# Moving weight splitting to VectorE, folding epsilon into a 65th column, and a third product tile for the conv

## The chip, the cores and the metric

The kernel runs on one core of one Trainium2 chip. The metric is the device time of one execution in microseconds (us). Before the change the runs took 1763.9, 1765.36 and 1767.11 us, with a median of 1765.36. The profiled execution took 1766.28 us, and its trace spans 1764.5 us from the first to the last instruction.

## The reference, cut to what matters

One block works on x of 1024 tokens by 1024 channels, in fp32. Four branches start from one normalised input:

```
h = rms_norm(x, g1);  z = h @ w_in            # 2048 glu, 3 x 1024 q k v, 2048 gate columns
a = a_val * sigmoid(a_gate)                    # glu
a = silu(rms_norm(causal_depthwise_conv(a, conv_w, conv_b), g))     # 31 taps
q = rms_norm(q per head of 64) * 64**-0.5;  k = rms_norm(k per head of 64)
o = dilated attention of q, k, v (16 heads, three dilations mixed)
x = x + (g_a * (a @ w_conv_out) + g_b * (o @ w_attn_out)) @ w_out
x = x + (silu(u_gate) * u_val) @ w_down        # u: conv of 3 taps of rms_norm(x) @ w_up
rms_norm(x, g) = x * rsqrt(mean(x * x) + 1e-6) * g
```

## The kernel before, in words

**Products in two halves.** A matrix product keeps fp32 precision by splitting each operand into a high part, rounded to the matmul type, and a low part, the rest. `split` (lines 78 to 81) does it: ScalarE copies the high part (line 80), and the engine that is passed as `by` subtracts to get the low part (line 81; VectorE where nothing is passed). Three matmuls then stand for one: high by high, high by low, low by high. `wsplit` (line 88) does this for weights. Weights come into a ring of four raw tiles named `raw` and leave as tiles `hi_...` and `lo_...`.

**The glu stage** (up to about 200 us) makes the 2048 glu columns in eight pairs of 128 value and 128 gate columns. Pairs 0 and 1 use plain products (`first_pair`, line 368). Pairs 2 to 7 use a scheme with seven instead of eight block products: the operands are sums and differences of blocks. VectorE forms those of the input once (lines 507 and 517 make the `forms` t1 to t4). For each pair, `pair_weights` (line 376) stages and splits the value weights, and `pair_sums` (line 385) makes four sums of 128x512 of the weights (line 390) and splits them. All this subtracting and adding is GpSimd's, as is the low part of pair 1's weights (line 494). `pair_first` and `pair_rest` (line 554) issue the products, through line 124 to 126, with the results named `uxz` and `uy`.

**The q, k and v stage** (about 175 to 475 us) makes six blocks of 512 columns, in order q, k, v, q, k, v, each over eight tiles of 128 tokens. A tile takes 24 matmuls (`gemm_tok`, line 144). For q and k `qkv_head` then does: ScalarE squares the tile (line 655), VectorE sums 64 squares for each of 8 heads (line 656), VectorE scales the sums by 1/64 and adds epsilon (line 104 in `rstd_of`), GpSimd raises to the power −1/2 (line 105), and VectorE scales the tile (line 659, tile `qn`). `qkv_tail`, three tiles later in the program, transposes on TensorE (line 667, `qt`), splits and stores. A v tile is split into a tile of a ring of four named `t4` and stored to HBM.

**The conv of 31 taps** runs beside that stage: six of eight channel blocks on VectorE (`by_dve`, line 624, one tap an instruction), two (3 and 6) as ScalarE products (line 615) that GpSimd adds up (line 616), with two product tiles in turn.

**What sets the order.** Each engine works through one queue in order. In a few places the order is the program's own (the manual schedules: the start, the attention, the change to the second half). Elsewhere, and so in the places of this change, a planner orders the instructions of each engine from a model of their costs (`schedule_with_timeline_sim` where the kernel is built).

Of the kernel before, what the change touches and what calls it, by code (L numbers as in the profile page):

```python
# [13 lines left out]
F32 = mybir.dt.float32  # L14
F32R = mybir.dt.float32r
AF = mybir.ActivationFunctionType
ALU = mybir.AluOpType
AX = mybir.AxisListType
# [3 lines left out]
P = 128  # L22
D = 1024
T = 1024
KT = D // P
H = 16
DH = 64
DFF = 2816
FT = DFF // P
CW = 31  # L30
FW = 3
EPS = 1e-6
# [21 lines left out]
def block_kernel(ctx: ExitStack, tc: tile.TileContext, x, g1, g2, pack, mask,  # L54
                 w_ch, w_qkv, w_co, w_ao, w_o, w_up, w_down, out):
    nc = tc.nc
    act, dve, pool, pe, sp = nc.scalar, nc.vector, nc.gpsimd, nc.tensor, nc.sync
# [17 lines left out]
    mhalf = cst.tile([P, 8], F32, name="mhalf")  # L75
    qkg = cst.tile([P, 1], F32, name="qkg")

    def split(hi, lo, src, by=dve):

        act.activation(hi, src, AF.Copy)  # L80
        by.tensor_tensor(out=lo, in0=src, in1=hi.bitcast(F32), op=ALU.subtract)  # L81
# [6 lines left out]
    def wsplit(src, name, by=dve):  # L88
        hi = wp.tile([P, 1024], F32R, tag="whi", bufs=4, name=f"hi_{name}")[:, : src.shape[1]]
        lo = wp.tile([P, 1024], F32R, tag="wlo", bufs=4, name=f"lo_{name}")[:, : src.shape[1]]  # L90
        split(hi, lo, src, by)
        return hi, lo
# [9 lines left out]
    def rstd_of(dst, ssq, n, tmp):  # L102

        dve.tensor_scalar(tmp, ssq, 1.0 / n, EPS, op0=ALU.mult, op1=ALU.add)
        pool.tensor_tensor(out=dst, in0=tmp, in1=mhalf[:, : tmp.shape[1]], op=ALU.pow)
# [23 lines left out]
    def four(t):  # L129
        return t.rearrange("p (a b) -> p a b", b=P)  # L130
# [166 lines left out]
    with tc.tile_pool(name="ph0", bufs=1, reuse_waits="tile") as p0:  # L297
# [77 lines left out]

        def pair_weights(c):
            v = stage(w_ch[c], f"v{c}")
            return v, wsplit(v, f"v{c}", pool)

        def pair_first(xz, w):  # L380
            for i, o in enumerate(xz):
# [3 lines left out]
        def pair_sums(c, v):  # L385
            g = stage(w_ch[8 + c], f"g{c}")
            s = wp.tile([P, 1024], F32, tag="raw", bufs=4, name=f"s12_{c}")
            a11, a12, a21, a22 = v[:, 0:512], v[:, 512:], g[:, 0:512], g[:, 512:]
            s1, s2 = s[:, 0:512], s[:, 512:]
            add_ = lambda o, a, b, op: pool.tensor_tensor(out=o, in0=a, in1=b, op=op)  # L390
            add_(s1, a21, a22, ALU.add)
            add_(s2, s1, a11, ALU.subtract)
            sw = wsplit(s, f"s12_{c}", pool)
            add_(a21, a11, a21, ALU.subtract)
            gw = wsplit(g, f"s3g_{c}", pool)
            add_(a12, a12, s2, ALU.subtract)
            return [four(t) for t in sw], [four(t) for t in gw], [four(t) for t in wsplit(a12, f"s4_{c}", pool)]

        ENG = mybir.EngineType
        HH, HL, LH = ((0, 0),), ((0, 1),), ((1, 0),)  # L400
        with tc.manual_schedule(engines={ENG.Activation, ENG.DVE, ENG.PE}):
            ps = [bank_ps(f"gb_{kk}") for kk in range(2)]
# [18 lines left out]
            wraw = [r for _, _, r in wfirst]  # L421
            names = [n for _, n, _ in wfirst]
            hl, wfirst = [], []
# [16 lines left out]
            a, b = range(4), range(4, 8)  # L440
# [49 lines left out]
        with tc.issue_after(ends[0].ins), tc.issue_after(ends[1].ins):  # L490
            for n in names[2:]:
                wtiles(n)
            for i in (2, 3):
                split(*hl[i], wraw[i], pool)
        for which in range(2):
            for half in range(2):
                glu.setdefault((1, half), []).append(bank_ps(f"glugv_1{half}{which}"))
# [79 lines left out]
        for c in range(2, 8):  # L577
# [3 lines left out]
            elif c + 1 < 8:  # L581
                v, w = pair_weights(c + 1)
# [4 lines left out]
    with tc.tile_pool(name="ph1", bufs=1, reuse_waits="tile") as p1, ExitStack() as rest:  # L587
        pc = rest.enter_context(tc.tile_pool(name="phc", bufs=1, reuse_waits="tile"))
        p1a_cm = tc.tile_pool(name="ph1a", bufs=1, side="right", reuse_waits="tile")
        p1a = p1a_cm.__enter__()  # L590
        t4 = lambda name, dt=F32: p1a.tile([P, 1024], dt, tag="t4", bufs=4, name=name)
        upper[0] = hb1.tile([P, 2, 4, 512], F32R, tag="hb01", name="b12_again")
        fetch(upper[0], db12)

# [2 lines left out]
        far = p1.tile([P, T], F32, name="prod0")  # L597
# [6 lines left out]

        def conv_branch():
            part = pc.tile([P, T], F32, name="part")
            prods = [far, pc.tile([P, T], F32, name="prod1")]
            w = lambda c, j: pk[:, C_CW + c * CW + j : C_CW + c * CW + j + 1]
            bias = lambda c: pk[:, C_CB + c : C_CB + c + 1]

            def by_pool(c):
                a = apad[c]
                act.activation(part, a[:, 0:T], AF.Identity, scale=w(c, 0), bias=bias(c))
                for j in range(1, CW):
                    act.activation(prods[j % 2], a[:, j : j + T], AF.Copy, scale=w(c, j))  # L615
                    pool.tensor_tensor(out=a[:, CW - 1 :] if j == CW - 1 else part, in0=prods[j % 2], in1=part,  # L616
                                       op=ALU.add)

            def by_dve(c):
                a = apad[c]  # L620
                work = psC.tile([P, T], F32, tag="C", name=f"work_{c}")
                dve.tensor_scalar(work, a[:, 0:T], w(c, 0), bias(c), op0=ALU.mult, op1=ALU.add)
                for j in range(1, CW):
                    dve.scalar_tensor_tensor(out=a[:, CW - 1 :] if j == CW - 1 else work, in0=a[:, j : j + T],  # L624
                                             scalar=w(c, j), in1=work, op0=ALU.mult, op1=ALU.add)
                return work

            def squares_in(c, sq):
                if c == 0:
                    act.activation(sqacc, apad[c][:, CW - 1 :], AF.Square)  # L630
                else:
                    act.activation(sq, apad[c][:, CW - 1 :], AF.Square)
                    dve.tensor_tensor(out=sqacc, in0=sqacc, in1=sq, op=ALU.add)

            for c in range(8):
                if c in BY_POOL:
                    by_pool(c)
                else:
                    squares_in(c, by_dve(c))
            for i, c in enumerate(BY_POOL):  # L640
                squares_in(c, prods[i % 2])
            return [a[:, CW - 1 :] for a in apad]

        def qkv_head(ch, tt, ps):
            kind, g8 = ch % 3, ch // 3
            psv = ps.rearrange("p (h d) -> p h d", h=8)
            if kind == 2:
                vt = t4(f"v_{ch}_{tt}", F32R).rearrange("p (h s d) -> p h s d", h=8, s=2)
                split(vt[:, :, 0, :], vt[:, :, 1, :], psv)
                spill(dv[g8][:, :, tt, :], vt.rearrange("p h s d -> p h (s d)"))  # L650
                return None
            sq = p1a.tile([P, 512], F32, tag="sq", bufs=2, name=f"sq_{ch}_{tt}")
            ss = p1.tile([P, 8], F32, tag="ss8", bufs=4, name=f"ss8_{ch}_{tt}")
            rs = p1.tile([P, 8], F32, tag="rs8", bufs=4, name=f"rs8_{ch}_{tt}")
            act.activation(sq, ps, AF.Square)
            dve.tensor_reduce(out=ss, in_=sq.rearrange("p (h d) -> p h d", h=8), axis=AX.X, op=ALU.add)
            rstd_of(rs, ss, DH, ss)
            qn = p1a.tile([P, 512], F32, tag="qn", bufs=4, name=f"qn_{ch}_{tt}")
            dve.tensor_tensor(out=qn.rearrange("p (h d) -> p h d", h=8), in0=psv,
                              in1=rs.unsqueeze(2).to_broadcast([P, 8, DH]), op=ALU.mult)  # L660
            return ch, tt, qn
# [783 lines left out]
```

## Time and profile before

| | |
|---|---|
| median of three runs | 1765.36 us |
| profiled execution | 1766.28 us |
| span of its trace | 1764.5 us |
| VectorE's conv, line 624, 174 instructions into `work` | 223.4 us |
| GpSimd's conv additions, line 616, 58 into `part` | 140.3 us |
| GpSimd's powers on q and k, line 105, 32 instructions | 52.7 us |
| granted TensorE clock, mean | 0.997 |

The profile is one execution. Its engines are PE (TensorE's matmuls), PEld (its weight loads), DVE (VectorE), ACT (ScalarE), POOL (GpSimd) and SP (the queue that issues most transfers). A row of a group names the line of the kernel, the engine, the operation, output and input by the names of the program's tiles, their shapes and how often it ran. Then follow busy time, the mean of one in ns, and the idle time ahead of it with what ended that. A row of the timeline begins with start and duration in us.

### The profile page before, as it was taken

What the parts mean: (1) busy time and instruction counts of PE and PEld (TensorE: products, weight loads), DVE (VectorE), ACT (ScalarE), POOL (GpSimd) and SP (SyncE); (2) the same over time, 40 slices, a digit from 0 to 9 for tenths busy, and PEclk for the clock granted to TensorE, in tenths of its full rate; (3) what the DMA queues carried; (4) which work ended last, traced back from release to release, by engine and by line L of the source; (5) the groups of instructions that cost most, each with busy time, mean ns of one, the idle gap of its engine ahead of it and who ended that gap; (6) DMA issues with size and microseconds to landing.
All of it is one profiled execution on the core that took longest, in us unless ns stands there. A gap on an engine that the chain in (4) does not pass through costs nothing.

```text
span 1764.5 us, 22792 instructions
## 1 busy us (share of the span) xinstructions
PE 1738.0 (98%) x8176; PEld 1442.3 (82%) x8176; DVE 1301.8 (74%) x1768; ACT 864.0 (49%) x1338; POOL 472.5 (27%) x327
## 2 busy tenths in 40 slices
PE   8999999899999999999999999999999999999999
PEld 6778878788888888888888888888888888878877
DVE  8999999998346666667655564687776776789863
ACT  6333555545356666667564343454544544543431
POOL 4876899989212222222210000000000000000000
PEclk9999999999999999999999999999999999999999
DMA  5223545344685655568446567632222222498851
GB/s 232 75 93 110 195 126 172 103 132 122 197 266 161 179 153 163 163 179 241 141 138 220 180 238 269 214 120 84 84 84 84 82 86 84 130 343 317 289 173 48
DMA packets 149411, 285.38 MB, mean 162 GB/s; under 512 B 12081, under 2 KB 61361, under 8 KB 149042
## 3 DMA queue, kind: packets, MB, share of 16 engines
q1 hardware_dynamic: 148144, 281.82, 48.9%
q10 hardware_dynamic: 1154, 2.10, 0.3%
q8 instruction: 64, 1.05, 0.2%
q14 instruction: 49, 0.40, 0.1%
HBM read 204.19 MB, written 79.69 MB: 161 GB/s over the span
## 4 chain that ended last, share of the span: by engine, by line
PE 79%; DVE 15%; issue 3%; DMA 2%; ACT 1%; SPq 0%; DVEq 0%; ACTq 0%
DVE work L624 8%; PE qkv L144 7%; PE dx L1281 6%; PE xz L124 6%; PE xz L126 6%; PE xz L125 6%; PE wo L144 5%; PE dy L1281 4%; PE pp L780 3%; PE gate L116 3%; PE gate L118 3%; PE gate L117 3%; PE y L126 2%; PE y L124 2%; PE y L125 2%
## 5 line engine op out<-in xcount | busy, mean ns | idle before, releaser
L624 DVE SCALAR_TENSOR_TENSOR work<-apad,pk,work 128x1024 f32<-128x1024 f32 x174 | 223.4, 1284 | 3.1
L774 POOL TENSOR_SCALAR p<-p,st 128x128 f32<-128x128 f32 (+7 forms) x128 | 97.0, 758 | 315.0 <-DVE st L773 218.8
L81 DVE TENSOR_TENSOR pl<-pp,ph 128x512 fp32r<-128x512 f32 x192 | 100.8, 553 | 87.8 <-ACT ph L80 87.6
L80 ACT ACTIVATE ph<-pp 128x512 fp32r<-128x512 f32 x192 | 87.1, 489 | 120.9 <-PE pp L780 118.0
L616 POOL TENSOR_TENSOR part<-prod,part 128x1024 f32<-128x1024 f32 x58 | 140.3, 2420 | 5.2 <-ACT prod L615 2.1
L765 DVE CUSTOM_DVE_ANT_0 p<-s,m 128x128 f32<-128x128 f32 (+7 forms) x128 | 96.4, 753 | 45.1 <-PE s L761 40.4
L144 PE MATMUL qkv<-hi_qkv,hT 128*128 128x512 f32 x384 | 115.6, 393 | 0.0
L1184 DVE SCALAR_TENSOR_TENSOR u<-u,pk 128x1023 f32<-128x1023 f32 x88 | 112.2, 1277 | 1.0 <-ACT u L1182 0.7
L770 ACT ACTIVATE p<-p,st 128x128 f32<-128x128 f32 (+7 forms) x128 | 99.2, 775 | 4.5 <-DVE st L765 3.5
L615 ACT ACTIVATE prod<-apad,pk 128x1024 f32<-128x1024 f32 x60 | 68.8, 1150 | 52.1 <-POOL part L616 52.0
L780 PE MATMUL pp<-ident,p 128*128 128x128 f32 x576 | 83.9, 272 | 0.0
L144 PEld LDWEIGHTS qkv<-hi_qkv,hT 128*128 128x128 f32 x384 | 71.6, 188 | 14.6
L81 DVE TENSOR_TENSOR lo_uv<-raw_uv,hi_uv 128x1024 fp32r<-128x1024 f32 x20 | 24.5, 1226 | 79.6 <-ACT hi_uv L80 79.6
L780 PEld LDWEIGHTS pp<-ident,p 128*128 128x128 f32 x576 | 70.1, 140 | 15.3
L144 PE MATMUL wo<-hi_wo,mT 128*128 128x512 f32 x256 | 80.1, 391 | 0.0
L794 PE MATMUL o<-ph,v 128*128 128x512 f32 x192 | 74.8, 393 | 0.9 <-DVE op L806 0.9
L124 PE MATMUL xz<-blk_t,hi_s3g 128*128 128x512 f32 x176 | 68.7, 390 | 0.7 <-ACT xc L1158 0.7
L124 PE MATMUL xz<-h2left,hi_uv 128*128 128x512 f32 x176 | 68.6, 390 | 0.0
L125 PE MATMUL xz<-blk_t,hi_s3g 128*128 128x512 f32 x176 | 68.5, 389 | 0.0
L126 PE MATMUL xz<-h2left,lo_uv 128*128 128x512 f32 x176 | 68.5, 389 | 0.0
L125 PE MATMUL xz<-h2left,hi_uv 128*128 128x512 f32 x176 | 68.5, 389 | 0.0
L126 PE MATMUL xz<-blk_t,lo_s3g 128*128 128x512 f32 x176 | 68.5, 389 | 0.0
(390 smaller groups left out, 5161.0 us busy)
## 6 DMA issues: line engine op xcount, KB each, us to landing
wr<-w_down SPq DMA_DIRECT2D x45, 512.0 KB, 5.5
gr<-dff SPq DMA_DIRECT2D x62, 256.0 KB, 5.2
raw_qkv<-w_qkv SPq DMA_DIRECT2D x24, 512.0 KB, 3.8
dff<-u SPq DMA_DIRECT2D x22, 512.0 KB, 2.6
raw_uv<-w_up SPq DMA_DIRECT2D x21, 512.0 KB, 3.2
raw_ug<-w_up SPq DMA_DIRECT2D x20, 512.0 KB, 3.2
dv<-v SPq DMA_DIRECT2D x16, 512.0 KB, 3.6
raw_gt<-w_ch SPq DMA_DIRECT2D x16, 512.0 KB, 5.4
```

The costliest lines, as they stand in the source:

```text
L81: by.tensor_tensor(out=lo, in0=src, in1=hi.bitcast(F32), op=ALU.subtract)
L124: pe.matmul(o, wh[:, k, :], bh[:, k, :], start=(start and k == 0), stop=False, skip_group_check=not start)
L125: pe.matmul(o, wh[:, k, :], bl[:, k, :], start=False, stop=False, skip_group_check=not start)
L126: end = pe.matmul(o, wl[:, k, :], bh[:, k, :], start=False, stop=(k == 3), skip_group_check=not start)
L144: pe.matmul(ps, l, r[:, k % 2, :], start=(n == 1), stop=(n == 3 * KT))
L616: pool.tensor_tensor(out=a[:, CW - 1 :] if j == CW - 1 else part, in0=prods[j % 2], in1=part, op=ALU.add)
L624: dve.scalar_tensor_tensor(out=a[:, CW - 1 :] if j == CW - 1 else work, in0=a[:, j : j + T], scalar=w(c, j), in1=work, op0=ALU.mult, op1=A ...
L770: act.activation(pt, pt, AF.Exp, bias=st[:, 0:1], scale=-1.0, accum_out=st[:, 1:2])
L774: pool.tensor_scalar(pt, pt, st[:, 2:3], 1.0, op0=ALU.mult, op1=ALU.mult)
L780: pe.transpose(pp[:, qb * P : (qb + 1) * P], pts[qb][:, kt * P : (kt + 1) * P], ident)
L1184: dve.scalar_tensor_tensor(out=acc[:, d:], in0=src[:, : T - d], scalar=w(2 - d), in1=acc[:, d:], op0=ALU.mult, op1=ALU.add)
L1281: pe.matmul(banks[n], a[:, c], b[:, d], start=(start and i == 0 and m == 0), stop=(stop and i == nf - 1 and m == 2), skip_group_check=True)
```

## The change

1. The low parts of the weights of pair 1 (tiles 2 and 3 of the first four), of the value weights of pairs 2 and 3, and all sums and splits of pair 2 are computed on VectorE instead of GpSimd. Pairs 4 to 7, and the sums of pair 3, stay on GpSimd.
2. The squares of a q or k tile go into one of two tiles that have a 65th column for each head, filled once with epsilon by GpSimd. ScalarE squares x/8 instead of x, so the sum over 65 columns is the mean of the squares plus epsilon. The scale-and-add on VectorE (line 104) is no longer there for q and k.
3. The conv's products on ScalarE go round three tiles instead of two. The ring `t4` for v has three tiles instead of four.

```diff
-            return v, wsplit(v, f"v{c}", pool)
+            return v, wsplit(v, f"v{c}", dve if c < 4 else pool)
...
-            add_ = lambda o, a, b, op: pool.tensor_tensor(out=o, in0=a, in1=b, op=op)
+            by = dve if c == 2 else pool
+            add_ = lambda o, a, b, op: by.tensor_tensor(out=o, in0=a, in1=b, op=op)
...
-            sw = wsplit(s, f"s12_{c}", pool)
+            sw = wsplit(s, f"s12_{c}", by)
...
-            gw = wsplit(g, f"s3g_{c}", pool)
+            gw = wsplit(g, f"s3g_{c}", by)
...
-            return [four(t) for t in sw], [four(t) for t in gw], [four(t) for t in wsplit(a12, f"s4_{c}", pool)]
+            return [four(t) for t in sw], [four(t) for t in gw], [four(t) for t in wsplit(a12, f"s4_{c}", by)]
...
-                split(*hl[i], wraw[i], pool)
+                split(*hl[i], wraw[i])
...
-        t4 = lambda name, dt=F32: p1a.tile([P, 1024], dt, tag="t4", bufs=4, name=name)
+        t4 = lambda name, dt=F32: p1a.tile([P, 1024], dt, tag="t4", bufs=3, name=name)
...
-            prods = [far, pc.tile([P, T], F32, name="prod1")]
+            prods = [far, *(pc.tile([P, T], F32, name=f"prod{i}") for i in (1, 2))]
...
-                    act.activation(prods[j % 2], a[:, j : j + T], AF.Copy, scale=w(c, j))
-                    pool.tensor_tensor(out=a[:, CW - 1 :] if j == CW - 1 else part, in0=prods[j % 2], in1=part,
+                    act.activation(prods[j % 3], a[:, j : j + T], AF.Copy, scale=w(c, j))
+                    pool.tensor_tensor(out=a[:, CW - 1 :] if j == CW - 1 else part, in0=prods[j % 3], in1=part,
                                        op=ALU.add)
...
+        sqs = [p1a.tile([P, 8, DH + 1], F32, name=f"sq_{i}") for i in range(2)]
+        for t in sqs:
+            pool.memset(t[:, :, DH:], EPS)
...
-            sq = p1a.tile([P, 512], F32, tag="sq", bufs=2, name=f"sq_{ch}_{tt}")
+            sq = sqs[tt % 2]
...
-            act.activation(sq, ps, AF.Square)
-            dve.tensor_reduce(out=ss, in_=sq.rearrange("p (h d) -> p h d", h=8), axis=AX.X, op=ALU.add)
-            rstd_of(rs, ss, DH, ss)
+            act.activation(sq[:, :, :DH], psv, AF.Square, scale=DH ** -0.5)
+            dve.tensor_reduce(out=ss, in_=sq, axis=AX.X, op=ALU.add)
+            pool.tensor_tensor(out=rs, in0=ss, in1=mhalf, op=ALU.pow)
```

## The prediction

> **What bounds the kernel now.** First the page's totals: TensorE is busy for 1738.0 of 1764.5 us, so only its idle time, and time in which its clock is held down, can be won.
>
> ```profile
> span 1764.5 us, 22792 instructions
> ...
> PE 1738.0 (98%) x8176; PEld 1442.3 (82%) x8176; DVE 1301.8 (74%) x1768; ACT 864.0 (49%) x1338; POOL 472.5 (27%) x327
> ```
>
> Second, TensorE's waits. (Columns: who waited for whom, total us, times, longest.) The first row is the transposes of q and k waiting for the normalised tile; the rows named uxz belong to block pairs 2 and 3.
>
> ```profile
> PE qt L667 <- DVE qn L659: 8.6, 5, 5.1
> ...
> PE uxz L124 <- DVE uring L567: 1.4, 1, 1.4
> PE uxz L124 <- ACT hi_s L80: 1.3, 1, 1.3
> PE uxz L126 <- POOL lo_s L81: 1.1, 1, 1.1
> ...
> PE uxz L124 <- ACT uring L560: 0.7, 1, 0.7
> ...
> PE qt L667 <- DVE ql L81: 0.2, 1, 0.2
> ```
>
> Third, the busy time by stretches: in two stretches of the q/k stage TensorE idles, and the granted clock (the column after POOL) falls to 0.97 and 0.93.
>
> ```profile
> 250.00:300.00 50.00, 47.51 (x218) 38.66 (x217) 49.22 (x54) 21.42 (x29) 44.84 (x22) 0.97 0.40 127
> 350.00:400.00 50.00, 46.26 (x210) 38.00 (x211) 48.09 (x54) 23.34 (x29) 42.63 (x22) 0.93 0.39 116
> 450.00:500.00 50.00, 50.00 (x236) 41.87 (x235) 15.91 (x29) 14.72 (x24) 5.72 (x3) 1.00 0.76 204
> ```
>
> Fourth, TensorE in order of time at those waits (start, duration; in brackets the wait before).
>
> ```profile
> 62.94 0.39 PE L124 MATMUL uxz<-hT,hi_v 128*128 128x512 f32 x1
> ...
> 63.39 0.39 PE L126 MATMUL uxz<-hT,lo_v 128*128 128x512 f32 x1
> ...
> 81.71 0.50 PE L124 MATMUL uxz<-ht,hi_s 128*128 128x512 f32 x1 [1.26 <-ACT hi_s L80]
> ...
> 254.62 0.66 PE L667 MATMUL qt<-ident,qn 128*128 128x128 f32 x4 [1.94 <-DVE qn L659]
> 255.00 0.71 PE L144 MATMUL qkv<-hi_qkv,b_again 128*128 128x512 f32 x1
> ...
> 353.08 1.12 PE L667 MATMUL qt<-ident,qn 128*128 128x128 f32 x4 [5.08 <-DVE qn L659]
> 353.85 0.78 PE L144 MATMUL qkv<-hi_qkv,b_again 128*128 128x512 f32 x1
> ...
> 357.41 0.67 PE L144 MATMUL qkv<-hi_qkv,b_again 128*128 128x512 f32 x2
> ```
>
> The normal pitch is (63.39 − 62.94) / 2 = 0.225 us. After the 5.08 us wait eight matmuls take 357.41 − 353.85 = 3.56 us instead of 1.8, so the clock costs 1.75 us more, and 0.4 us on the four transposes. The 1.94 us wait is followed by the same double pitch; I charge it the same 1.75 us. The 1.26 us wait at 81.71 sits in a stage whose clock stays full. The Trainium skill (TensorE: Matmul & The Clock Gate, part 1) has the clock throttled only after an idle window of about 3.4 us; by that the wait of 1.94 us would cost itself alone and the sum below would be 1.75 us smaller. The trace disagrees.
>
> So the ceiling: in the q/k stage 8.6 + 0.2 us of waits and 3.9 us of clock, 12.7 us; in pairs 2 and 3 1.4 + 1.3 + 1.1 + 0.7 = 4.5 us; together 17.2 us, which leads to 1748.2 us. The other waits lie at the start or behind 900 us, where nothing is edited.
>
> **Part 1, the weights.** Eleven subtractions and additions leave GpSimd: six of 128x1024 (low parts of g1, v1, v2, v3, and of pair 2's sums and differences) and five of 128x512 (four sums of pair 2 and the last low part).
>
> ```profile
> 31.00:76.00 45.00, 40.94 (x12) 1.00 0.26 100
> ...
> 30.00:67.00 37.00, 37.00 (x164) 30.62 (x164) 36.97 (x15) 14.88 (x15) 35.21 (x9) 1.00 0.22 86
> ```
> ```profile
> 31.56 2.28 DVE L507 TENSOR_TENSOR plain_xa<-b 128x2048 f32<-128x2048 f32 x1
> 33.76 4.48 DVE L507 TENSOR_TENSOR r<-hT,hT 128x2048 f32<-128x2048 f32 x1
> ...
> 73.27 2.29 DVE L507 TENSOR_TENSOR ht<-plain_xa,ht 128x2048 fp32r<-128x2048 f32 x1 [1.38 <-ACT ht L517]
> 75.48 0.69 DVE L487 TENSOR_TENSOR sg<-glugv,sg 128x512 f32<-128x512 f32 x1
> ```
> ```profile
> L81 DVE TENSOR_TENSOR lo_uv<-raw_uv,hi_uv 128x1024 fp32r<-128x1024 f32 x20 | 24.5, 1226 | 79.6 <-ACT hi_uv L80 79.6
> ...
> L180 DVE TENSOR_TENSOR lo_gt<-raw_gt,hi_gt 128x512 fp32r<-128x512 f32 x12 | 7.8, 688 | 9.6 <-ACT hi_gt L187 9.5
> ```
>
> The first row is the busy time of line 507 alone: twelve operations, 40.9 us. Before GpSimd starts (31.56) and after it stops (73.27) one takes 2.28 us, beside it up to 4.48. In that time GpSimd is busy 35.21 us with nine of the eleven. Alone the twelve would take 12 × 2.28 = 27.4, so VectorE gets 13.5 us back. The moved work costs it 6 × 1.226 + 5 × 0.688 = 10.8 us. VectorE is then through this list 2.7 us earlier than its present 76.1, though it does more.
>
> What that does to the waits: the 0.7 us (ScalarE's copy of X, queued behind the form that waits for VectorE) goes. The 1.3 and 1.1 us are pair 3's sums, which stay on GpSimd but now find it idle.
>
> ```profile
> 77.91 1.29 POOL L390 TENSOR_TENSOR s<-raw_g 128x512 f32<-128x512 f32 x1
> ```
> ```profile
> raw_g<-w_ch SPq DMA_DIRECT2D x8, 512.0 KB, 3.6
> ```
>
> They start at 77.91, and must come some 1.3 us earlier. Their weights can be loaded when pair 2's sums have been split; on VectorE I place that near 70 (31.56 + 27.4 + five low parts 6.1 + gate products and sums about 4), and 3.6 us of load gives 74, so both waits go. The 1.4 us behind VectorE's conv work I leave. New: v2's low part, needed at 63.39, now queues on VectorE with the forms. Bounds: nothing if it slips between them; if it follows all twelve and g1's and v1's low parts, it ends at 31.56 + 27.4 + 3 × 1.23 + two gate products 1.4 = 64.1, and with the 1.38 us gap and v3 ahead of it 66.7, 3.3 us late. I take 0.5, since the gap of 1.38 us ahead of the last form has room for it. Part 1: 3.1 − 0.5 = 2.6 us, between −0.2 and 4.5.
>
> **Part 2, the epsilon column.** It removes 32 scale-and-add operations (line 104) from VectorE between ScalarE's squares and GpSimd's power. The scale goes into the squaring, at no cost; each reduction reads 520 for 512 elements, 1.6% of the 0.69 us below, 0.01 us; two small memsets join GpSimd's queue, in an idle spot.
>
> ```profile
> L104 DVE TENSOR_SCALAR ss<-ss x32: 153/564/2345, 198.9 to 430.3; 128x8 f32<-128x8 f32 x32
> ```
> ```profile
> 250.97 1.72 DVE L104 TENSOR_SCALAR ss<-ss 128x8 f32<-128x8 f32 x1
> ...
> 342.55 0.69 DVE L656 TENSOR_REDUCE ss<-sq 128x8 f32<-128x512 f32 x1 [0.98 <-ACT sq L655]
> ...
> 344.34 2.19 DVE L104 TENSOR_SCALAR ss<-ss 128x8 f32<-128x8 f32 x1
> ...
> 350.09 2.35 DVE L104 TENSOR_SCALAR ss<-ss 128x8 f32<-128x8 f32 x1
> 352.35 0.68 DVE L659 TENSOR_TENSOR qn<-qkv,rs 128x512 f32<-128x512 f32 x1
> ```
> ```profile
> 336.61 9.89 POOL L616 TENSOR_TENSOR part<-prod,part 128x1024 f32<-128x1024 f32 x4
> 346.61 1.65 POOL L105 TENSOR_TENSOR rs<-ss,mhalf 128x8 f32<-128x8 f32 x1
> ...
> 350.07 2.34 POOL L616 TENSOR_TENSOR part<-prod,part 128x1024 f32<-128x1024 f32 x1
> ```
>
> An operation on eight elements takes 0.15 us at least and 2.35 at most, and its long cases end where a GpSimd addition ends (346.5, 352.4): it is held until GpSimd is done, and holds what is queued behind it. At 353 that is the very tile TensorE waits for. Replayed without it: the reduction ends at 343.24, GpSimd's four additions still run to 346.5, the power ends at 348.3, the scaling 0.68 later at 348.9, and TensorE, out of work since 353.08 − 5.08 = 348.0, waits 1.0 instead of 5.08, too short for the clock to fall. At 254 the 1.72 us come off a wait of 1.94. The other three waits sum to 1.6, each behind such an operation, and about 0.3 stays. Left: 1.0 + 0.2 + 0.3 + 0.2 = 1.7, so the replay saves 12.7 − 1.7 = 11.0. What is late next is GpSimd's power behind its additions. The order of each queue is planned anew, so between the 11.0 and half the ceiling (6.3) I take 9.5, near the replay.
>
> **Part 3, the third product tile.** It frees ScalarE to run two products ahead, and leaves three buffers for v instead of four.
>
> ```profile
> L616 POOL TENSOR_TENSOR part<-prod,part 128x1024 f32<-128x1024 f32 x58 | 140.3, 2420 | 5.2 <-ACT prod L615 2.1
> ```
> ```profile
> dv<-v SPq DMA_DIRECT2D x16, 512.0 KB, 3.6
> ```
>
> GpSimd waits for products 2.1 us in all, off TensorE's path: nothing. A tile of v takes 24 matmuls, 5.4 us, and its store 3.6; three buffers cover 16 us. Nothing, at worst 2 us at the head of a v block, where tiles come in a burst.
>
> **Sum.** 2.6 + 9.5 = 12.1 us off the span of 1764.5, so 1752.4; the execution's own 1766.28 becomes 1754.2. It lay 0.9 above the median of the runs, 1765.36, so the forecast is 1753.3.
>
> **The rivals.** *GpSimd is next*: with line 104 gone the power still queues behind additions of 2.4 us, and half the q/k stage's 12.7 stays: 2.6 + 6.3 = 8.9 off, 1756.5; with part 1 at nothing 1759. For it: GpSimd is busy 44.84 of 50 us; against it: the replay. *The lock*: pair 3's sums on GpSimd fall beside VectorE's moved subtractions. These are then stretched as line 507 is; four of them, each held for one GpSimd operation of 2.4 us, cost 9.6, less the 2.7 won above: VectorE is 6.9 us later than now, part 1 turns into 2.6 − 6.9 = −4.3, and 5.2 us come off in all, 1760.2. The Trainium skill (SBUF — State Buffer, Who interferes with whom) says just this of a VectorE operation with two SBUF inputs beside a GpSimd one that reads SBUF. The 4.48 us row bears the rule out; against the case, GpSimd has only pair 3 left there. *No change*: the waits come back at other places, as the planned order shifts, 1762 to 1768. *Slower*: the transposes are planned earlier. The order is worked out from modelled costs; with one operation less in the chain a transpose may be put ahead of matmuls that cover it now, while the power behind its additions is as slow as before. A head of a q or k block then costs what 353 costs, 5.08 + 2.15 = 7.2 us; all four 28.9 against 12.7 now, 16.2 lost and 2.6 won: 1779. It decides from 12.7 + 2.6 = 15.3 us on, a little over two such heads. Against it: three of the four heads wait under 2 us now.
>
> **How the numbers follow.** Forecast 0.49 (1748.2, the ceiling, to 1756), GpSimd next 0.18, the lock 0.09, no change 0.12, slower 0.12. About 0.2% (3.5 us) is what a measurement here can tell. The first three cases are faster by more: 0.76; same 0.12; slower 0.12. The range runs from the ceiling less 1 us for the spread of runs, 1747.2, to 1765, which takes in the lock and half of no change.
>
> **What would show it.** Right: no line 104 on q and k; line 507 at 2.3 us throughout; the waits for qn under 3 us in all with the clock at 1.00 from 250 to 400; no uxz waits for hi_s and lo_s. Wrong: the qn row as large as before, with GpSimd's power ending last; TensorE waiting near 63 for lo_v; VectorE operations of 128x1024 over 2 us near 75; ScalarE waiting for stores of v.

## The result and the profile after

The changed kernel takes 1747.08 us (median of 4 runs, 1745.71 to 1748.42). The kernel before took 1765.3 us beside it. The ratio is 0.9896 with a 95% interval of 0.9879 to 0.9913. So 18.2 us are gone where 12.1 were forecast, and the time lies 0.1 us below the low end of the predicted range.

The profiled execution took 1745.71 us, the lowest of its four runs, while that of before, 1766.28, lay 1 us above its median. Between the two profiles the difference is therefore 20.6 us instead of 18.2.

The totals of the page of after:

```profile
span 1743.7 us, 22762 instructions
...
PE 1731.3 (99%) x8176; PEld 1440.1 (83%) x8176; DVE 1278.6 (73%) x1747; ACT 867.2 (50%) x1338; POOL 435.6 (25%) x318
```

TensorE's waits in after begin as follows (who waited for whom, total us, times, longest):

```profile
PE tp L349 <- DVE xs L341: 3.0, 2, 2.2
PE gb L405 <- DMA gb<-g: 2.2, 1, 2.2
PE o L799 <- DVE op L811: 1.5, 1, 1.5
```

No row with qn, ql or uxz is left; these three lie at the start (tp, gb) and in the attention (o), where nothing was edited. The same two stretches of the q/k stage as in the prediction: TensorE (the first column after the length) is busy all the time, and the granted clock (after POOL's column) stays at 1.00.

```profile
250.00:300.00 50.00, 50.00 (x236) 41.39 (x235) 45.01 (x48) 27.06 (x34) 49.45 (x23) 1.00 0.52 160
350.00:400.00 50.00, 50.00 (x238) 41.32 (x237) 47.35 (x52) 26.09 (x33) 48.79 (x25) 1.00 0.45 137
```

Where did the time come from? Two marks bracket everything that was edited: the first matmul into `uxz` (pair 2), and the first into `pss`, once the q, k and v stage is over. Rows of the two tiles, before and then after (the two times at the end are the first and last start):

```profile
L124 PE MATMUL uxz<-hT,hi_v x48: 389/389/389, 62.9 to 168.5; 128*128 128x512 f32 x48
```
```profile
L724 PE MATMUL pss<-ones,sqacc x16: 164/250/250, 489.3 to 490.9; 128*128 128x1 f32 x16
```
```profile
L124 PE MATMUL uxz<-hT,hi_v x48: 389/389/389, 62.5 to 159.7; 128*128 128x512 f32 x48
```
```profile
L729 PE MATMUL pss<-ones,sqacc x16: 164/250/250, 469.4 to 471.0; 128*128 128x1 f32 x16
```

The stretch between the marks is 489.3 − 62.9 = 426.4 us before and 469.4 − 62.5 = 406.9 us after. Of the 20.8 us by which the spans differ, 19.5 are won here, 0.4 ahead of the first mark and 0.9 behind the second. This stretch (called the marked stretch below) is a cleaner measure than the whole time, and each kernel is given by both. The waits in the last column are the sums of the rows for this stretch.

| kernel | median us | marked stretch us | TensorE's waits in it: us, times |
|---|---|---|---|
| before | 1765.3 | 426.4 | 13.3, 10 |
| after: all three parts | 1747.08 | 406.9 | none |
| part 1 alone | 1759.89 | 420.6 | 9.6, 6 |
| part 2 alone | 1753.6 | 414.4 | 5.0, 4 |
| part 3 alone | 1765.95 | 426.5 | 12.9, 9 |
| parts 1 and 2 | 1748.27 | 406.9 | none |
| parts 1 and 3 | 1760.12 | 420.3 | 9.1, 6 |
| after, four low parts back on GpSimd | 1752.54 | 412.4 | 3.2, 3 |
| after, pair 2's sums back on GpSimd | 1749.09 | 408.5 | 1.3, 1 |
| after, a second reduction for epsilon | 1752.01 | 411.5 | 2.6, 1 |
| after, an unread scale-and-add aside | 1770.1 | 430.5 | 14.9, 8 |
| after, an unread reduction aside | 1747.57 | 406.9 | none |
| before, additions halved | 1767.78 | 425.2 | 14.6, 9 |

### The profile page after: what moved, and what is told of

It reads as the page before. It is cut to its first block, busy times and chain, and to the rows that moved or that the text cites. A ratio compares the mean times of both kernels' runs of the same rounds, so it can differ in the third digit from the quotient of the medians.

```text
span 1743.7 us, 22762 instructions
## 1 busy us (share of the span) xinstructions
PE 1731.3 (99%) x8176; PEld 1440.1 (83%) x8176; DVE 1278.6 (73%) x1747; ACT 867.2 (50%) x1338; POOL 435.6 (25%) x318
## 4 chain that ended last, share of the span: by engine, by line
PE 98%; DMA 1%; ACT 0%; DVE 0%; POOL 0%; SPq 0%; issue 0%; DVEq 0%; ACTq 0%
PE qkv L144 15%; PE dx L1286 7%; PE xz L124 6%; PE xz L126 6%; PE xz L125 6%; PE dy L1286 5%; PE wo L144 5%; PE gate L116 4%; PE pp L785 4%; PE gate L118 3%; PE gate L117 3%; PE glugv L372 3%; PE y L126 2%; PE y L125 2%; PE y L124 2%; PE s L766 2%
## 5 line engine op out<-in xcount | busy, mean ns | idle before, releaser
L144 PEld LDWEIGHTS qkv<-hi_qkv,hT 128*128 128x128 f32 x384 | 71.5, 188 | 14.6
L144 PE MATMUL qkv<-lo_qkv,hT 128*128 128x512 f32 x192 | 69.3, 392 | 0.0
L124 PE MATMUL xz<-h2left,hi_uv 128*128 128x512 f32 x176 | 68.7, 390 | 0.0
```

What stands on the lines that cost most here:

```text
L124: pe.matmul(o, wh[:, k, :], bh[:, k, :], start=(start and k == 0), stop=False, skip_group_check=not start)
L144: pe.matmul(ps, l, r[:, k % 2, :], start=(n == 1), stop=(n == 3 * KT))
```

## The experiments

**Each part alone.** Part 1 alone is the kernel before with the weights on VectorE:

```diff
-            return v, wsplit(v, f"v{c}", pool)
+            return v, wsplit(v, f"v{c}", dve if c < 4 else pool)
...
-            add_ = lambda o, a, b, op: pool.tensor_tensor(out=o, in0=a, in1=b, op=op)
+            by = dve if c == 2 else pool
+            add_ = lambda o, a, b, op: by.tensor_tensor(out=o, in0=a, in1=b, op=op)
...
-                split(*hl[i], wraw[i], pool)
+                split(*hl[i], wraw[i])
```

> Part 1 alone. My theory (each part removes its own waits): the four uxz waits of 4.5 us go, with about 0.28 us for each wait in which the matmul pipeline runs empty and refills, so some 5.6 us: about 1759.7 us, with the q/k waits for qn still 7 to 10 us and the clock still below 1.00 there. Rival (a lighter VectorE early on is what counts): the qn waits shrink as well, under 4 us, and the time is near 1751. Rival (the planned order decides, by chance): any value, with uxz waits in it.

It took 1759.89 us, a ratio of 0.9962 (0.9948 to 0.9976) to the kernel before, 6.4 us off. Among its waits no uxz is left, while those for qn stay:

```profile
PE qt L668 <- DVE qn L660: 8.8, 5, 6.3
```

Part 2 alone is the kernel before with the epsilon column:

```diff
...
-            act.activation(sq, ps, AF.Square)
-            dve.tensor_reduce(out=ss, in_=sq.rearrange("p (h d) -> p h d", h=8), axis=AX.X, op=ALU.add)
-            rstd_of(rs, ss, DH, ss)
+            act.activation(sq[:, :, :DH], psv, AF.Square, scale=DH ** -0.5)
+            dve.tensor_reduce(out=ss, in_=sq, axis=AX.X, op=ALU.add)
+            pool.tensor_tensor(out=rs, in0=ss, in1=mhalf, op=ALU.pow)
```

> Part 2 alone. My theory: the qn waits of 8.8 us go, the 3.9 us of clock and some 1.6 us of refilling with them, 14.3 us: about 1751 us, with the four uxz waits unchanged near 4.5 us. Rival (GpSimd's power is next): qn waits of 3 us or more are left, 1755 to 1758.

It took 1753.6 us, 0.9928 (0.9913 to 0.9942), 12.7 us off where 14.3 were expected. Now the mirror image: no wait for qn is left, and the four of pairs 2 and 3 are still there.

```profile
PE uxz L124 <- DVE uring L567: 1.8, 1, 1.8
PE uxz L124 <- ACT hi_s L80: 1.3, 1, 1.3
...
PE uxz L126 <- POOL lo_s L81: 1.1, 1, 1.1
...
PE uxz L124 <- ACT uring L560: 0.8, 1, 0.8
```

The longest of them is 1.8 us instead of 1.4, and here the clock falls behind it, to 0.97 (the column after POOL) from 50 to 100 us, where before it stays at 1.00:

```profile
50.00:100.00 50.00, 45.13 (x189) 35.90 (x188) 47.23 (x31) 15.76 (x18) 37.15 (x20) 0.97 0.22 74
```

Part 3 alone is the third product tile and the smaller ring of v:

```diff
-        t4 = lambda name, dt=F32: p1a.tile([P, 1024], dt, tag="t4", bufs=4, name=name)
+        t4 = lambda name, dt=F32: p1a.tile([P, 1024], dt, tag="t4", bufs=3, name=name)
...
-            prods = [far, pc.tile([P, T], F32, name="prod1")]
+            prods = [far, *(pc.tile([P, T], F32, name=f"prod{i}") for i in (1, 2))]
...
-                    act.activation(prods[j % 2], a[:, j : j + T], AF.Copy, scale=w(c, j))
+                    act.activation(prods[j % 3], a[:, j : j + T], AF.Copy, scale=w(c, j))
...
```

> Part 3 alone, with three buffers for v. My theory: no change, 1764 to 1767 us, all waits as before. Rival (ScalarE's queue, blocked by a product that waits for GpSimd, is part of the q/k latency): the qn waits shrink by half and the time is near 1759.

It took 1765.95 us, 0.9999 (0.999 to 1.0009). The waits for qn are there as before:

```profile
PE qt L667 <- DVE qn L659: 8.4, 5, 4.8
```

The other way round, the change without part 3:

```diff
-        t4 = lambda name, dt=F32: p1a.tile([P, 1024], dt, tag="t4", bufs=3, name=name)
+        t4 = lambda name, dt=F32: p1a.tile([P, 1024], dt, tag="t4", bufs=4, name=name)
...
-            prods = [far, *(pc.tile([P, T], F32, name=f"prod{i}") for i in (1, 2))]
+            prods = [far, pc.tile([P, T], F32, name="prod1")]
...
-                    act.activation(prods[j % 3], a[:, j : j + T], AF.Copy, scale=w(c, j))
+                    act.activation(prods[j % 2], a[:, j : j + T], AF.Copy, scale=w(c, j))
...
```

> Parts 1 and 2 without part 3, v with four buffers. My theory: as the full change, 1746 to 1748.5 us. Rival (ScalarE's queue): some qn waits come back, 1750 or more.

It took 1748.27 us, 0.9897 (0.9883 to 0.9912), with the marked stretch of after, 406.9. So part 3 is worth nothing that can be measured here, alone or beside the others, and the gain belongs to parts 1 and 2. Each removes its own waits. The waits that stay are together a little longer than before: 9.6 + 5.0 = 14.6 us against 13.3.

**Which half of part 1.** One kernel is after with the low parts of g1, v1, v2 and v3 back on GpSimd, so that only pair 2's sums are on VectorE:

```diff
-            return v, wsplit(v, f"v{c}", dve if c < 4 else pool)
+            return v, wsplit(v, f"v{c}", pool)
...
-                split(*hl[i], wraw[i])
+                split(*hl[i], wraw[i], pool)
```

> The full change, but the low parts of g1, v1, v2 and v3 stay on GpSimd; only pair 2's sums and their splits are on VectorE. My theory (pair 3's sums find GpSimd free earlier): no uxz waits for hi_s and lo_s, 1746 to 1750 us, though line 507's operations are stretched again while GpSimd splits. Rival (the stretching of VectorE is what cost the pairs their waits): waits of 2 us or more in pairs 2 and 3, 1750 or more.

It took 1752.54 us, 0.9926 (0.9911 to 0.994), above the expected 1746 to 1750; marked stretch 412.4. The waits for `hi_s` and `lo_s` are gone as expected, but one wait at the block pairs is there, behind VectorE, and two short ones for qn (1.1 us in all):

```profile
PE uxz L124 <- DVE uring L568: 2.1, 1, 2.1
```

VectorE's second form, at 34.34, is stretched to 4.48 us again, beside GpSimd's low parts.

The other kernel is after with pair 2's sums back on GpSimd:

```diff
-            by = dve if c == 2 else pool
+            by = pool
```

> The full change, but pair 2's sums and their splits stay on GpSimd; only the four low parts are on VectorE. My theory: pair 3's sums queue behind pair 2's on GpSimd again, as before, but all of it starts some 15 us sooner; the waits for hi_s and lo_s shrink from 2.4 to under 1.5 us, 1747 to 1750. Rival (stretching): as VectorE is stretched by the sums, waits of 2 us or more, 1750 or more.

It took 1749.09 us, 0.9909 (0.9892 to 0.9926), marked stretch 408.5. It has no uxz wait, and one wait of 1.3 us in the stretch:

```profile
PE qkv L144 <- DMA b_again<-db: 1.3, 1, 1.3
```

GpSimd starts pair 3's sums at 68.57 here, though it has pair 2's ahead of them:

```profile
68.57 3.22 POOL L391 TENSOR_TENSOR s<-raw_g 128x512 f32<-128x512 f32 x1
```

VectorE's forms are stretched here too, beside GpSimd's sums and splits:

```profile
66.16 4.47 DVE L508 TENSOR_TENSOR plain_xa<-plain_xa,plain_xb 128x2048 f32<-128x2048 f32 x1
```

Either half removes the waits for `hi_s` and `lo_s`. The low parts of four weights are the larger half: with them off GpSimd only 2.0 us separate the kernel from after, and its one wait, for a load at 200 us, lies in the q, k and v stage. The stretching of the forms is not what decides. Line 508 takes 33.0 us of VectorE in the first of these kernels and 33.3 in the second (27.9 in after), and the second has no wait at the pairs. What the 2.1 us of the first hang on was not separated: its conv on VectorE starts at 78.15, after 2.51 us of waiting for GpSimd to fill the edge of a conv tile, and six conv steps stand directly ahead of the sum that TensorE waits for.

**What in part 2 does it.** Removing the scale-and-add does two things: VectorE's queue is no longer held until a GpSimd addition ends, and the chain from the squares to `qn` is one step shorter, also for the planner. The change without part 2 is the starting point:

```diff
...
-            act.activation(sq[:, :, :DH], psv, AF.Square, scale=DH ** -0.5)
-            dve.tensor_reduce(out=ss, in_=sq, axis=AX.X, op=ALU.add)
-            pool.tensor_tensor(out=rs, in0=ss, in1=mhalf, op=ALU.pow)
+            act.activation(sq, ps, AF.Square)
+            dve.tensor_reduce(out=ss, in_=sq.rearrange("p (h d) -> p h d", h=8), axis=AX.X, op=ALU.add)
+            rstd_of(rs, ss, DH, ss)
```

> Parts 1 and 3, line 104 back. My theory (an operation on eight elements is held until GpSimd's running instruction ends, and holds VectorE's queue): as part 1 alone, about 1760 us, line 104 up to 2.3 us long and the waits for qn back at 7 to 10 us. Rival (the third product tile helps here): under 1756.

It took 1760.12 us, 0.9968 (0.9956 to 0.9979), the same as part 1 alone, with the waits for qn:

```profile
PE qt L668 <- DVE qn L660: 8.3, 5, 6.0
```

The next kernel keeps the long chain but puts a reduction in place of the scale-and-add. The sum goes into a pair whose second element is epsilon, and a second, tiny reduction adds the two:

```diff
...
-            dve.tensor_reduce(out=ss, in_=sq, axis=AX.X, op=ALU.add)
+            dve.tensor_reduce(out=pair[:, :, 0:1], in_=sq.rearrange("p (h d) -> p h d", h=8), axis=AX.X, op=ALU.add)
+            dve.tensor_reduce(out=ss, in_=pair, axis=AX.X, op=ALU.add)
```

> The full change, but the epsilon comes in by a second VectorE operation: the squares are summed over 64 columns into a pair (sum, epsilon), and a second, tiny reduction adds the two. The chain has as many VectorE operations as before the change, and none is a scale-and-add. My theory (the hold behind GpSimd was the cost): as the full change, 1746 to 1749 us, the tiny reduction 0.1 to 0.2 us each time, no waits for qn over 1 us. Rival (the length of the chain and its place in VectorE's queue were the cost): waits for qn of 4 us or more, 1753 to 1760.

It took 1752.01 us, 0.9923 (0.9906 to 0.9939), between the two theories. The tiny reductions are not held (the group's total and the mean in ns behind the bar):

```profile
L663 DVE TENSOR_REDUCE ss<-pair 128x8 f32<-128x16 f32 x32 | 4.9, 160 | 0.0
```

One wait for qn is left, on TensorE's timeline:

```profile
339.80 0.81 PE L674 MATMUL qt<-ident,qn 128*128 128x128 f32 x4 [2.58 <-DVE qn L666]
```

Two things lie behind it. On GpSimd's timeline four additions are planned ahead of the power, where after has three (shown further down):

```profile
325.57 9.86 POOL L617 TENSOR_TENSOR part<-prod,part 128x1024 f32<-128x1024 f32 x4
335.38 3.26 POOL L664 TENSOR_TENSOR rs<-ss,mhalf 128x8 f32<-128x8 f32 x2
```

The first of the two powers ends at 335.38 + 3.26 / 2 = 337.0, against 334.2 in after. Then VectorE has one more step of its conv planned ahead of the scaling (at 337.86), which starts 2 us behind the power (0.5 us in after):

```profile
339.06 0.68 DVE L666 TENSOR_TENSOR qn<-qkv,rs 128x512 f32<-128x512 f32 x1
```

Now the opposite: after's short chain, with an unread scale-and-add of the same eight numbers put beside it, so that only its place in VectorE's queue counts.

```diff
             pool.tensor_tensor(out=rs, in0=ss, in1=mhalf, op=ALU.pow)
+            aside = p1.tile([P, 8], F32, tag="as8", bufs=4, name=f"as8_{ch}_{tt}")
+            dve.tensor_scalar(aside, ss, 1.0, EPS, op0=ALU.mult, op1=ALU.add)
```

> The full change, with a scale-and-add on the eight sums put back beside the chain: it reads them, writes a tile that nobody reads, and nothing waits for it. So VectorE's queue has the old operation with its hold, and the chain from squares to transpose is as short as in the change. Two theories are left for the 12 to 13 us of part 2: the hold behind GpSimd, and the length of the planned chain, by which GpSimd's power is put one addition earlier. The second reduction without a hold kept 1 wait of 2.6 us and cost 4.9 us. Hold alone: the operation is up to 2.3 us long, some waits for qn come back, 1751 to 1757 us. Chain alone: no waits, 1747 us, though the holds are there.

It took 1770.1 us, 1.0023 (1.0011 to 1.0034): all that parts 1 and 2 had won is lost to an operation that nobody reads. That is 13 us past the upper end of what was expected, so its control was run too: the same kernel with an equally unread reduction in that place. The planned order of the two is the same on TensorE, ScalarE and GpSimd, and on VectorE but for the kind of this operation; on SP one weight load stands elsewhere.

```diff
-            dve.tensor_scalar(aside, ss, 1.0, EPS, op0=ALU.mult, op1=ALU.add)
+            dve.tensor_reduce(out=aside, in_=ss.unsqueeze(2), axis=AX.X, op=ALU.add)
```

> The same kernel as the one with the unread scale-and-add beside the chain, with that operation replaced by an equally unread reduction of the same eight numbers (128x8 into 128x8). The planned order is the same on TensorE, and on VectorE the same but for the kind of this operation, so the pair of kernels differs in the hold alone. Hold: reductions were not held before (160 ns each), so about 31 operations of 0.16 us (5 us in all, 33 with the scale-and-add), no waits for qn of more than 2 us in all, 1747 to 1750 us. Rival, the planned order: what the scale-and-add beside the chain cost comes from the operation standing in VectorE's queue and from transposes planned otherwise, whatever its length; then the waits for qn and ql stay near 14 us and the time near 1766 to 1770.

It took 1747.57 us, 0.9885 (0.9867 to 0.9903), with the marked stretch of after, 406.9, and no wait in it. With the planned order equal, the hold alone costs 1770.1 − 1747.57 = 22.5 us (430.5 − 406.9 = 23.6 in the marked stretch). The two groups (shortest, median and longest in ns), first the scale-and-add, then the reduction:

```profile
L664 DVE TENSOR_SCALAR as<-ss x32: 155/321/2358, 193.9 to 434.5; 128x8 f32<-128x8 f32 x32
```
```profile
L664 DVE TENSOR_REDUCE as<-ss x32: 148/152/156, 194.2 to 411.9; 128x8 f32<-128x8 f32 x32
```

In the kernel with the scale-and-add one can watch the hold make a wait. VectorE's timeline, then GpSimd's, then TensorE's:

```profile
253.03 2.35 DVE L664 TENSOR_SCALAR as<-ss 128x8 f32<-128x8 f32 x1
...
257.14 2.15 DVE L664 TENSOR_SCALAR as<-ss 128x8 f32<-128x8 f32 x1
259.20 1.27 DVE L666 TENSOR_TENSOR qn<-qkv,rs 128x512 f32<-128x512 f32 x2
```
```profile
252.92 2.42 POOL L617 TENSOR_TENSOR part<-prod,part 128x1024 f32<-128x1024 f32 x1
255.31 1.64 POOL L662 TENSOR_TENSOR rs<-ss,mhalf 128x8 f32<-128x8 f32 x1
256.92 2.33 POOL L617 TENSOR_TENSOR part<-prod,part 128x1024 f32<-128x1024 f32 x1
```
```profile
260.02 1.08 PE L674 MATMUL qt<-ident,qn 128*128 128x128 f32 x4 [4.77 <-DVE qn L666]
```

Each of the two held operations begins just after an addition has begun and ends with it: 253.03 + 2.35 = 255.38 against 252.92 + 2.42 = 255.34, and 257.14 + 2.15 = 259.29 against 256.92 + 2.33 = 259.25. The factor for `qn` was ready at 255.31 + 1.64 = 256.95, but the scaling starts at 259.20, behind the second hold, and TensorE waits 4.77 us.

Last, the hold shortened instead of removed: the kernel before with GpSimd's additions cut in two of 512 columns.

```diff
-                    pool.tensor_tensor(out=a[:, CW - 1 :] if j == CW - 1 else part, in0=prods[j % 2], in1=part,
-                                       op=ALU.add)
+                    for s in HALVES:
+                        o = a[:, CW - 1 :] if j == CW - 1 else part
+                        pool.tensor_tensor(out=o[:, s], in0=prods[j % 2][:, s], in1=part[:, s], op=ALU.add)
```

> The kernel before, with each conv addition on GpSimd cut in two of 512 columns, about 1.3 us each. If line 104 is held until GpSimd's running instruction ends, its longest case falls from 2.35 to some 1.3 us (2.4 where a weight split runs), its sum from 28.7 to some 18 us, and the waits for qn shrink to 3 to 6 us: 1755 to 1763. If the hold has another cause, the longest cases stay near 2.3 beside the additions and the time is 1764 to 1768.

It took 1767.78 us, 1.0011 (0.9996 to 1.0025): no gain, against the expected 1755 to 1763. The holds did follow GpSimd's instruction: their sum fell from 28.7 to 18.4 us, as expected, and the longest from 2345 ns to 1615, but the waits for qn did not shrink:

```profile
L104 DVE TENSOR_SCALAR ss<-ss x32: 154/610/1615, 197.9 to 427.9; 128x8 f32<-128x8 f32 x32
```
```profile
PE qt L668 <- DVE qn L660: 10.1, 5, 3.9
```

The longest hold is one beside a weight split, which was not halved; it ends with the split (VectorE's timeline, then GpSimd's). Beside a halved addition of 1.3 us the longest is 1.24 us, at 409.99.

```profile
276.90 1.61 DVE L104 TENSOR_SCALAR ss<-ss 128x8 f32<-128x8 f32 x1
```
```profile
276.08 2.40 POOL L81 TENSOR_TENSOR lo_qkv<-raw_qkv,hi_qkv 128x1024 fp32r<-128x1024 f32 x1 [0.95 <-ACT hi_qkv L80]
```

The additions themselves grew from 140.3 us to 148.2, and the order was planned anew. Which of the two kept the waits was not separated. The profiled execution is the fastest of ten, 4 us below the median; its marked stretch is 1.2 us shorter than before's.

**The theories on part 2.** The five kernels with parts 1 and 3 in place stand like this:

| | chain planned short | chain planned long |
|---|---|---|
| no hold | 1747.1 (after), 1747.6 (reduction aside) | 1752.0 (second reduction) |
| hold | 1770.1 (scale-and-add aside) | 1760.1 (without epsilon) |

That the shorter chain alone explains part 2 is refuted by the reduction and the scale-and-add aside: same order, same chain, 22.5 us apart. As long as the hold is there, neither plan comes below 1760. How the 13 us divide depends on the way one goes, and only the two kernels of equal order price one thing alone. With the hold taken out first, it is worth some 8 us (1760.1 − 1752.0) and the shorter chain the other 5 (1752.0 − 1747.1), each between plans that differ; at the tile shown, the planner puts the power behind three additions instead of four, and the scaling behind one conv step less. With the chain shortened first, the kernel gets 10 us slower (1770.1 against 1760.1), and the hold is worth 22.5. That a closer plan loses more to a hold would explain this; it was not tried further.

## Why the prediction was right in direction and short in size

**Right.** The direction, the hold in part 2, GpSimd's relief in part 1, and part 3. All but one on its list of signs were seen: no line 104 on q and k, no waits for qn, the clock at 1.00, no waits for `hi_s` and `lo_s`; line 507 was to stay at 2.3 us throughout, and its last operation takes 3.01. Line 508 (507 before) alone, twelve operations from 30 to 73 us of after:

```profile
30.00:73.00 43.00, 27.92 (x12) 1.00 0.34 123
```

That is 27.9 us; the prediction had 27.4, from 40.9. That VectorE gets this time back is right, but the waits did not need it: the kernel with 33.3 us there has none at the pairs.

What came short was the size, in three terms. The forecast of 12.1 is the ceiling of 17.2 less 1.4 + 0.5 in part 1 and 1.7 + 1.5 in part 2. All of these 5.1 us were won as well, and the ceiling itself was 2.3 too low; 12.1 + 5.1 + 2.3 = 19.5 is the gain in the marked stretch. By the medians the gain is 18.2, which is above the ceiling too; the range began at the ceiling less 1 us, so it had no room for more.

**The ceiling of 17.2 us was too low.** It priced a wait at its idle row and added the clock only where it fell. TensorE's timeline of before, around the row at 81.71 that the prediction shows:

```profile
80.07 0.39 PE L126 MATMUL uy<-ht,lo_s 128*128 128x512 f32 x1
...
82.05 0.40 PE L125 MATMUL uxz<-ht,hi_s 128*128 128x512 f32 x1
```

From 80.07 to 81.71 are 1.64 us, 1.41 more than the pitch of 0.23, where the row says 1.26; the next pitch, 0.34, is 0.11 too long as well. The wait costs 1.52 us in all. The kernel with pair 2's sums back on GpSimd agrees: one wait of 1.3 us, and a marked stretch 408.5 − 406.9 = 1.6 us longer than after's. The ten waits of before, 13.3 us by their rows, cost 19.5. Of the 6.2 us between, the prediction had 3.9 as clock; the other 2.3 come to about a quarter of a microsecond a wait, as at 81.71. What makes this surcharge is not shown here.

The clock term itself was in order. The kernel with the second reduction has one wait of 2.58 us, followed by transposes of 0.81 us that take 0.60 in after, and its marked stretch is 411.5 − 406.9 = 4.6 us longer; its granted clock is 0.97 from 300 to 350 us. The Trainium skill (TensorE: Matmul & The Clock Gate, part 1) wants an idle window of about 3.4 us before the clock is throttled; this wait stays under it and still costs 2 us beyond itself, so here the measurement decides against it once more. The length of a wait alone does not tell whether the clock falls. Behind 1.8 us it fell in the kernel with part 2 alone, and behind 2.28 us in the kernel with halved additions (TensorE's timeline, then the stretch) it stayed at 1.00:

```profile
254.97 0.63 PE L668 MATMUL qt<-ident,qn 128*128 128x128 f32 x4 [2.28 <-DVE qn L660]
```
```profile
250.00:300.00 50.00, 45.83 (x217) 37.45 (x216) 49.18 (x58) 23.92 (x30) 47.52 (x32) 1.00 0.41 121
```

**Part 1 was forecast at 2.6 and is worth 5.8** (marked stretch, 426.4 − 420.6; 6.4 by the medians). Two steps failed: "The 1.4 us behind VectorE's conv work I leave", and the 0.5 for v2's low part. VectorE's timeline of after shows why the second cost nothing:

```profile
33.16 2.29 DVE L508 TENSOR_TENSOR r<-hT,hT 128x2048 f32<-128x2048 f32 x1
...
40.43 1.22 DVE L81 TENSOR_TENSOR lo_v<-raw_v,hi_v 128x1024 fp32r<-128x1024 f32 x1
...
44.37 1.22 DVE L81 TENSOR_TENSOR lo_v<-raw_v,hi_v 128x1024 fp32r<-128x1024 f32 x1
...
68.76 3.01 DVE L508 TENSOR_TENSOR ht<-plain_xa,ht 128x2048 fp32r<-128x2048 f32 x1
71.70 1.77 DVE L81 TENSOR_TENSOR lo_s<-raw_v,hi_s 128x512 fp32r<-128x512 f32 x1
```

The low parts of v2 and v3 are slipped between the forms; the first is done at 41.65, some 20 us before TensorE wants v2's. VectorE is through the list at 71.70 + 1.77 = 73.47, by 2.7 us earlier than the 76.17 of before (75.48 + 0.69), just as the prediction had it; but it did not ask what this gives to the conv work behind the list, and there the 1.4 us went. The sum that TensorE waits for (line 567, 568 after) starts at 93.51 before, with twelve conv steps planned ahead of it, and at 82.68 in after, with six:

```profile
93.51 0.68 DVE L567 TENSOR_TENSOR uring<-uxz,up 128x512 f32<-128x512 f32 x1
```
```profile
82.68 0.69 DVE L568 TENSOR_TENSOR uring<-uxz,up 128x512 f32<-128x512 f32 x1
```

Pair 3's sums start earlier than the estimate as well, at 66.96 instead of about 74, on GpSimd's timeline:

```profile
66.96 1.30 POOL L391 TENSOR_TENSOR s<-raw_g 128x512 f32<-128x512 f32 x1 [40.99 <-DVE lo_s3g L81]
```

With the four waits gone the surcharge of each goes too, about 1 us of the 5.8.

**Part 2 was forecast at 9.5 and is worth 12.0** (426.4 − 414.4; 12.7 by the medians). The step that failed is what was left in: the replay kept 1.7 us of waits, and the forecast then took 1.5 more off the gain because the order is planned anew. The replay held the order of before, with four additions ahead of the power. After has three; GpSimd's timeline, VectorE's and TensorE's at the same tile:

```profile
325.20 7.39 POOL L617 TENSOR_TENSOR part<-prod,part 128x1024 f32<-128x1024 f32 x3
332.56 1.65 POOL L662 TENSOR_TENSOR rs<-ss,mhalf 128x8 f32<-128x8 f32 x1
```
```profile
331.15 0.69 DVE L661 TENSOR_REDUCE ss<-sq 128x8 f32<-128x520 f32 x1 [2.02 <-ACT sq L660]
...
334.74 0.69 DVE L664 TENSOR_TENSOR qn<-qkv,rs 128x512 f32<-128x512 f32 x1
```
```profile
336.68 0.60 PE L672 MATMUL qt<-ident,qn 128*128 128x128 f32 x4
```

The scaled tile is there at 335.43, and the transposes start at 336.68 with no wait. So planning anew helped, where it was counted as a risk. Part 1 and part 2 together give 19.5 in the marked stretch, 1.7 more than 5.8 + 12.0. Of that, 1.3 are the waits that grow when a part stands alone (14.6 against 13.3); the other 0.4 were not traced. On top of part 1, part 2 is worth 420.6 − 406.9 = 13.7.

**The rivals.** *GpSimd is next* did not come: GpSimd is fuller than before (49.45 of 50 us from 250 on) and TensorE has no wait left that leads to it. With the second reduction it was part of one, at one tile. *The lock* has its mechanism and not its price: the last form takes 3.01 us and the last low part 1.77 instead of 2.28 and 0.69, beside pair 3's sums, 1.8 us in all instead of 9.6. *Slower* needed transposes planned earlier than the power can follow, and the change has no such wait. The kernel with the scale-and-add aside comes near it, with 1770.1 us: planned for the short chain, with the hold still there. The plan alone is not the cause, for without the hold it takes 1747.6.

## What to carry to other kernels

Price a wait of TensorE at its idle row plus a surcharge, read off the starts of the matmuls around one wait before setting a ceiling, and look at the granted clock behind it. When a tiny operation on a vector engine now and then takes many times its shortest time, look at what ends with it on the neighbour engine, and fold it into an operation of a kind that is not held rather than moving it aside. To price a hold, replace the operation by one that is not held and leave the planned order as it is.

## What the runs showed of the hardware

A VectorE scale-and-add over 128x8, 0.15 us when alone, is held for up to 2.36 us until GpSimd's running addition or weight split ends, and it holds whatever is queued behind it, read or unread; beside additions halved to 1.3 us the longest hold is 1.24 us. Beside GpSimd's power of 1.65 us it was not held: before's at 233.90 takes 0.16 us inside the power from 233.30 to 234.96. A reduction of the same size in the same place takes 0.148 to 0.156 us in all 32 cases. The Trainium skill (SBUF — State Buffer, Who interferes with whom) says that `tensor_scalar` can take the pair of ports that VectorE shares with GpSimd, and that `tensor_reduce` on trn2 never contends; both agree with these rows. What had not been expected is the price of so small an operation: 22.5 us of a kernel.
